# A layer's scale and shift, summed beside the mixers of the layer before

## The chip, the cores and the metric

The kernel runs on one core of a Trainium2 chip. The metric is the device time of one execution, in microseconds (us). TensorE is called PE here, VectorE DVE, ScalarE ACT, GpSimd POOL; SP is the engine whose queue issues all the loads and stores.

## The reference

Two layers of a small diffusion-style model in float32 work on 640 tokens of 2048 channels: 128 of a prompt ("context") and 512 of a sample. Every layer first modulates its input with a scale and a shift that come from a condition vector, one for the prompt and one for the sample, then mixes, then adds the gated output projection:

```python
def adaln(x, cond, norm_w, w_ada, b_ada):
    mod = jax.nn.silu(cond) @ w_ada + b_ada
    shift, scale, gate = jnp.split(mod, 3, axis=-1)
    return rmsnorm(x, norm_w) * (1 + scale) + shift, gate

for li in range(DEPTH):                        # 2
    hc, gate_c = adaln(xc, cc, norm_w[li], w_ada[li], b_ada[li])
    hl, gate_l = adaln(xl, cl, norm_w[li], w_ada[li], b_ada[li])
    if li % 2 == 0:
        ...                                    # mixers A (gated delta rule) and B (windowed attention)
    else:
        ...                                    # mixers C (gated linear attention) and D (neighbourhood attention)
    xc = xc + gate_c * (oc @ w_out)
    xl = xl + gate_l * (ol @ w_out)
```

`w_ada` of a layer is 2048 x 6144: 2048 columns each of shift (part 0), scale (part 1) and gate (part 2). Its product with two condition vectors depends on no token, so it can be made at any time before its use.

## The kernel before

The activations stand channel by channel: 16 tiles of [128 channels, 640 tokens], each split into a high and a low part (`hh`, `hl`), as every weight is (`w_hi`, `w_lo`), so that three fast products make one exact one. A projection's column tile takes 16 K-tiles x 3 products x 2 halves of 320 tokens. Its weights come in quarters of four K-tiles (256 KB, `weights`, L1048): loaded into `w_st`, rounded by ACT to `w_hi` (L1051), subtracted by DVE to `w_lo` (L1053), three quarters ahead.

The stages, in order of time: the start (norm and modulation of layer 0), the layer 0 mixers with their projections, the first out projection, the layer 1 mixers with theirs, the second out projection.

In the layer 0 mixers, `run` steps generators side by side: the inverses, scans, preparation, values, gates of mixer A, queries and heads of mixer B, and `gate`, which makes part 2 of layer 0's modulation with products of PE (`ada`). A generator yields the time that its next products have to wait (in a clock that the program itself counts, `self.now`) or a condition; the earlier in the list, the sooner served. Between them `Main` fills in a few products of a projection. PE's order is pinned to this program order (`keep_in_program_order`); the other engines' order is made by the framework's scheduler (`schedule_with_timeline_sim=True`). In mixer A, each of 8 heads needs small triangular inverses, made by a chain of small POOL instructions (`a_invert`, L489 to L497) between two trips through DRAM; `a_inverted` loads them back (L517 to L519), and `a_join` uses them first (`i_vps`). Then comes a scan over 10 chunks (tiles `a_st`, `a_s`, `a_vno`), whose steps go back and forth between PE, ACT and DVE.

`ada_vec` makes a part of the modulation without PE doing the big sum. For every K-tile of 128 rows it loads [128, width] of `w_ada` (L1308), and for either condition adds the tile times one number per row to a sum: as one DVE instruction (L1322; L1320 for the first K-tile), or as a product of ACT (L1325) that POOL adds (L1327). After 16 K-tiles, small products of PE sum over the partitions (`adv_ps`), DVE copies the result (L1338), `ada_out` turns it (`ada_t`) and puts it into place (`mod`). With width 512 a part has 4 groups of 16 steps.

In the first out projection, `out_proj` takes 16 column tiles; after each, DVE adds the gated product to the residual (L1521), ACT squares it (L1464), POOL sums the squares (L1465), and POOL multiplies by layer 1's scale as soon as that is known (`scaled`, L1425). Beside it run two `ada_vec` streams for layer 1, a step of both after every sixth (later third) piece of the projection: the scale (part 1), one condition on DVE and one on ACT and POOL, and the shift (part 0), both on DVE. `end` then norms, scales and shifts, and makes layer 1's `hh` and `hl` (L1764, L1765). Layer 1's gate (part 2) is made beside the layer 1 mixers by `ada_vec` with width 256, both conditions on DVE and a wait of 6 a step.

Of the kernel before, what the change touches and what calls it, by code (L numbers as in the profile page):

```python
# [13 lines left out]
PSUM = bass.MemoryType.PSUM  # L14
# [5 lines left out]
T = 640  # L20
# [5 lines left out]
# ---------------------------------------------------------------- host constants (shapes only)  # L26
# [24 lines left out]
def gate_table():  # L51
    """Sums over a chunk: to the row itself, for either orientation of a block, and over one half."""
    P = np.arange(128)
    half = P // 64
    same = (half[:, None] == half[None, :]).astype(np.float32)
    F = (P[:, None] <= P[None, :]) * same
    B = (P[:, None] >= P[None, :]) * same
    h0 = (half == 0)[:, None]
    t = [np.where(h0, F, B), np.where(h0, B, F), np.repeat(h0, 128, 1), np.repeat(~h0, 128, 1)]
    return np.ascontiguousarray(np.concatenate(t, 1).astype(np.float32))  # L60


# what goes with the constants: widths
# [8 lines left out]
class G:  # L72
    """What every part of the kernel shares."""

    def mm(self, out, lhsT, rhs, **kw):
        """A matrix product, kept behind the one before; self.now runs along with TensorE's time (us)."""
# [13 lines left out]
def rsqrt(g, pool, x, n, tag, bufs=1):  # L90
    """1/sqrt(x) by Newton steps on VectorE; x is [.., n], positive."""
    nc = g.nc
# [12 lines left out]
# ---------------------------------------------------------------- mixer A: gated delta rule  # L105
CP = 648          # 2 | 128 | 4 | 512 | 2
CL = 644          # 128 | 4 | 512


def a_tok(blk, half):  # L110
    """First token of the chunk in one half of a block: context chunks 0, 1; latent chunks b, 7 - b."""
    if blk == 0:
        return 64 * half
    return 128 + 64 * (blk - 1 if half == 0 else 8 - blk)


def by_block(lat, half):
    """[128, 4, 64] view, of [128, 512] latent columns in token order, of the chunks in one half of blocks 1-4."""
    v = lat.rearrange("p (b c) -> p b c", c=64)
    return v[:, 0:4] if half == 0 else v[:, 7:3:-1]  # L120


def a_gates(g, src, tri):
    """beta, g and their cumulated forms for all heads; src: [128, 640] tile, 0:64 to be summed over two groups of
    32 rows (beta dir head | g dir head)."""
# [17 lines left out]
    # log1p(e) = 2 atanh(e / (2 + e))  # L143
# [39 lines left out]
    # with a row for every block and head, to be spread over the partitions  # L183
# [20 lines left out]
def a_conv(g, h, which, src):  # L204
    """Projected tile (two PSUM halves of 320) -> 2 silu(conv) as [128, 640], tokens block by block."""
# [22 lines left out]
def silu2(g, src, pool, tag="zs", bufs=1):  # L228
    """2 silu of a projected tile (two PSUM halves of 320) -> [128, 640]."""
# [10 lines left out]
def a_prep(g, h, qT, kT):  # L240
    """A delta-rule head up to the inverses of its chunks, both directions; q, k come doubled."""
# [6 lines left out]
    # ---- sums of squares per token  # L248
# [8 lines left out]
    def gram(x):  # L257
        """The second against the first within every chunk."""
# [19 lines left out]
    # ---- per-token scalars, [128, 2 orientations, 5 blocks]  # L278
# [21 lines left out]
    # ---- decays: exp(gc[col] - gc[row]) on the allowed side, and the other sign for the forward triangles  # L300
# [16 lines left out]
    # ---- grams  # L317
# [11 lines left out]
def a_scan(g, S, vT, gates, st):  # L329
    """The scan over a head's chunks and its norm; returns o^T [128, 640] gated."""  # L330
# [7 lines left out]
    def turn(x, dst):  # L338
        """Token-major x, in two parts."""
# [12 lines left out]
    # ---- what a chunk takes of a state: k against the inverses, for every block and orientation  # L352
# [20 lines left out]
    # ---- scan over chunks  # L373
# [9 lines left out]
    def ahead(o, blk, r, zero=False):  # L383
        """What of a chunk does not wait for the state."""
# [5 lines left out]
    def step(o, blk, s, p, nxt):  # L390
        """One chunk of either direction; s: [128, 2 directions, 128] states, None for zero states."""
# [53 lines left out]
    # ---- norm over the head, per token  # L445
# [28 lines left out]
def a_invert(g, M):  # L474
    """lhsT tiles for the inverses of I - M, M strictly lower (transposed for the forward units)."""
# [29 lines left out]
def a_inverted(g, h, d1, d2):  # L505
    """Loads what a_invert left: lhsT tiles for the inverses, their diagonal blocks as they are, and the blocks of M
    below them."""
# [17 lines left out]
def a_join(g, Mo, Zt, X, between):  # L525
    """The blocks of the inverses that couple the two halves of a chunk; between: products to do meanwhile."""
# [31 lines left out]
def a_setup(g, es):  # L558
    """Pools and fixed tiles of mixer A."""
# [9 lines left out]
# ---------------------------------------------------------------- attention, shared by mixers B and D  # L569
def attn_probs(g, q, keys, adds, init, sink):  # L570
    """Of one block of 128 queries: softmax(q^T keys + adds) / 2, [128 q, keys].
    keys: [(AP [128 d, n], n)]; adds: [(c0, c1, AP [128 q, c1 - c0])]."""
# [21 lines left out]
    # P / (2 den): the gate comes doubled  # L594
# [11 lines left out]
def attn_out(g, S, vals):  # L606
    """Returns, after yields, [128 d, 128 q] (PSUM) = V^T S; vals: [AP [128 keys, 128 d]]."""
# [14 lines left out]
def attn_run(g, blocks):  # L622
    """blocks: [(arguments of attn_probs, vals, function of the output)]; the scores run one block ahead."""
# [10 lines left out]
def drain(g, dst, src, scale=None):  # L634
    """Two PSUM halves of 320 tokens -> [128, 640]."""
# [8 lines left out]
def token_major(g, vT, dst, blocks):  # L644
    """PE-transposes 128-column views of vT into dst[:, i]."""
# [9 lines left out]
# ---------------------------------------------------------------- mixer B: windowed GQA, sink, axial rotary  # L655
def b_rope(g, x):
    """Rotates the latent columns of x [128, 640] in place."""
# [36 lines left out]
def b_head(g, h, q, gates):  # L694
    """Puts the outputs in the place of the queries."""
# [35 lines left out]
def b_table():  # L731
    """cos, signed sin [128 channels, 512 tokens]; window masks [128 q, prev | cur | cache | next]."""
# [13 lines left out]
# ---------------------------------------------------------------- mixer D: neighbourhood attention  # L746
# [18 lines left out]
def d_head(g, h, q, k, vsrc, gates):  # L765
    """Puts the outputs in the place of the queries, then of the gates."""
# [49 lines left out]
def d_table():  # L816
    """Column masks [128 q = (r, c), 4 blocks x 32 key columns] | 128 zeros."""
# [12 lines left out]
def d_rpb(rpb):  # L830
    """[8 heads, 15, 31] -> [8, 128 q = (r, c), 8 key rows x 48]: the entry for key row kr and key column
    16 + (key column - query column base) of every query, zero outside."""
# [8 lines left out]
# ---------------------------------------------------------------- mixer C: gated linear attention  # L841
# [3 lines left out]
def c_table():  # L845
    """tri/16 for either direction [128, 128]; 2 I [128, 64]; per level, the [128, 64] mask of the pairs (s on partitions,
    c along the row)."""
# [22 lines left out]
def c_head(g, h, qsrc, ksrc, vsrc, gates, st):  # L870
    """vsrc: two."""
    nc, c, P = g.nc, g.c, g.pc1
    hd = slice(h * 128, h * 128 + 128)
    # ---- log-decays, token-major, and their cumulated sums, channel-major
# [27 lines left out]
    # ---- scores within a chunk: the diagonal (counted by both directions), then halves against halves  # L902
# [9 lines left out]
    def decayed(l):  # L912
        """Queries and keys against the decay at the middle of their 2 w tokens: forward the later half's queries and the
        earlier half's keys, backward the others."""
# [27 lines left out]
    # ---- v, token-major  # L942
# [7 lines left out]
    # ---- decays to the chunk's ends  # L950
# [16 lines left out]
    # ---- states at the chunks' starts, and outputs; backward first  # L967
# [14 lines left out]
    def out_block(b, sf, sb):  # L982
        """sf, sb: the states at the starts of the block's two chunks, either direction."""
# [35 lines left out]
    # ---- norm over the head, per token  # L1019
# [22 lines left out]
# ---------------------------------------------------------------- trunk  # L1042
def weights(g, dram, k0, k1):
    """K-tiles k0 to k1, four at most, of one 128-column tile of a weight [128, 16 x 128], as exact high and low parts."""
# [12 lines left out]
def narrow(g, dram, q):  # L1057
    """Quarter q of the K-tiles of a 32-column tile of a weight [128, 16 x 32]: [128, 4, 64], low parts behind high ones."""
# [10 lines left out]
class Main:  # L1069
    """The projections asked for, a few products at a time; weights are loaded ahead."""  # L1070
# [7 lines left out]
    def ask(self, dram, prio, now=False, n=None):  # L1078
        """For use with yield from: out^T [128 columns, 640 tokens] of one weight tile, as two PSUM halves."""
# [12 lines left out]
    def turns(self, drams):  # L1092
        """Some, by quarters in turn, the first half of the tokens first; the second one in the general PSUM."""
# [11 lines left out]
    def halves(self, drams):  # L1105
        """The last ones, of all of them the first half of the tokens first."""
# [28 lines left out]
    def narrow(self, r, q, wt):  # L1135
        """Of one of 32 columns a quarter of the K-tiles; the sums of the weights' high and low parts stay apart."""
# [12 lines left out]
    def work(self, r, k0, w):  # L1149
        """The K-tiles from k0 on for which w are the weights."""  # L1150
# [18 lines left out]
    def when(self):  # L1169
        """The time from which there is something to do."""  # L1170
# [20 lines left out]
    def until(self, ask, fill=None, every=1):  # L1191
        """The result of one that was asked for, with a step of fill between so many of its pieces."""
# [12 lines left out]
def run(g, main, *streams):  # L1205
    """Runs generators side by side, the first ones first; they yield how long (us) their next products have to
    wait, or a condition. The projections fill the time."""
# [17 lines left out]
def split(g, x, k, lo=None):  # L1225
    """High and low parts of x [128, 640] in the slots of k-tile k; lo: where x is already in its low part's."""
# [8 lines left out]
# projections of layer 0 that start before all of the modulation is there  # L1235
EARLY = [0, 8, 41, 43, 33]
# the mixers' outputs in the order in which they are done
# [738 lines left out]
```

## Time and profile before

| | us |
|---|---|
| median of 3 runs (2844.3 to 2858.61) | 2854.96 |
| span of the profiled execution | 2851.8 |
| busy: PE | 2682.8 |
| busy: DVE | 1654.9 |
| busy: ACT | 987.1 |
| busy: POOL | 781.3 |
| mean granted clock of PE | 0.970 of full speed |

The profiled execution's own time is its span; it lies 3.2 us below the median of the runs. A profile of one execution shows each instruction of each engine with its start and its length, what ended the idle time before it, and the clock that PE was granted. Rows name the line of the kernel, the engine, the operation and the tiles (out<-in). PE's matrix products are pipelined and their ends are modelled, so the time from one start to the next says more of PE's pace than its busy time does.

### The profile page before, as it was taken

The page shows a single profiled execution, that of the slowest core. Times are in us where ns is not written, and L with a number is a line of the kernel's source. Part 1 is how long each engine was busy: PE and PEld are TensorE (multiplying, and loading weights), DVE is VectorE, ACT ScalarE, POOL GpSimd, SP SyncE. Part 2 cuts the span into 40 slices and gives each one's busy share as a digit, 9 for nine tenths or more (in the row PEclk, how much of TensorE's full clock was granted, in tenths as well). Part 3 has the DMA queues.
Part 4 walks back from the last instruction along what each step waited for, and adds up shares of the span by engine and source line. Part 5 has one row for each costly group of instructions (what it writes and reads, how often), then busy time and mean ns, then how long its engine had stood idle before and what let it go on. Part 6 is the DMA issues. An engine that isn't in the chain of part 4 may idle for free.

```text
span 2851.8 us, 54254 instructions
## 1 busy us (share of the span) xinstructions
PE 2682.8 (94%) x20975; PEld 2464.5 (86%) x20975; DVE 1654.9 (58%) x3650; ACT 987.1 (35%) x2190; POOL 781.3 (27%) x930
## 2 busy tenths in 40 slices
PE   6979999999999999978889899999999999999997
PEld 5768788787888998978789898999799989979996
DVE  5665555556665754489997754446354535645225
ACT  3232342343333434343334542343233224324222
POOL 2325505134153350025553230022002001200223
PEclk9989999999999999998989999999999999999998
DMA  9933233232322221276663413223132313215223
GB/s 337 288 97 103 78 93 94 83 97 82 106 86 64 78 87 54 76 239 209 210 213 116 133 66 102 79 87 104 50 112 72 106 59 104 83 64 182 99 100 133
DMA packets 264705, 329.82 MB, mean 116 GB/s; under 512 B 76013, under 2 KB 148925, under 8 KB 264447
## 3 DMA queue, kind: packets, MB, share of 16 engines
q1 hardware_dynamic: 264447, 326.35, 35.3%
q8 instruction: 165, 2.70, 0.4%
q14 instruction: 93, 0.76, 0.1%
HBM read 294.95 MB, written 28.68 MB: 113 GB/s over the span
## 4 chain that ended last, share of the span: by engine, by line
PE 69%; DVE 10%; issue 9%; DMA 7%; POOL 2%; ACT 1%; SPq 1%; DVEq 0%; ACTq 0%; POOLq 0%
PE acc L77 54%; PE a_st L77 3%; DVE vec L1322 2%; DMA a_df<-gc_d 2%; PE c_ops L77 2%; PE at_s L77 2%; PE at_o L77 2%; DVE w_lo L1053 1%; PE c_U L77 1%; DMA adv<-w_ada 1%; PE ada_ps L77 1%; DVE scale L1322 1%; DVE hl L1765 1%; PE at_pt L84 1%; DMA scale<-w_ada 1%
## 5 line engine op out<-in xcount | busy, mean ns | idle before, releaser
L77 PE MATMUL acc<-hh,w_hi 128*128 128x320 f32 (+1 forms) x4544 | 1462.4, 323 | 46.4 <-DVE x L1521 41.9
L77 PE MATMUL acc<-hl,w_hi 128*128 128x320 f32 (+1 forms) x4544 | 1424.3, 314 | 8.6 <-DVE hl L1231 8.0
L77 PE MATMUL acc<-hh,w_lo 128*128 128x320 f32 x4480 | 1408.3, 314 | 9.8 <-DVE w_lo L1053 9.5
L77 PEld LDWEIGHTS acc<-hh,w_hi 128*128 128x128 f32 (+1 forms) x4544 | 866.5, 191 | 96.7 <-issue 76.8
L77 PEld LDWEIGHTS acc<-hl,w_hi 128*128 128x128 f32 (+1 forms) x4544 | 867.5, 191 | 16.4 <-DVE hl L1231 11.5
L77 PEld LDWEIGHTS acc<-hh,w_lo 128*128 128x128 f32 x4480 | 857.0, 191 | 17.4 <-DVE w_lo L1053 10.8
L1053 DVE TENSOR_TENSOR w_lo<-w_st,w_hi 128x512 fp32r<-128x512 f32 x561 | 430.0, 767 | 531.9 <-ACT w_hi L1051 528.2
L1051 ACT CAST w_hi<-w_st 128x512 fp32r<-128x512 f32 (+1 forms) x604 | 365.0, 604 | 823.2 <-PE acc L77 684.5
L1322 DVE SCALAR_TENSOR_TENSOR vec<-vec,cond 128x256 f32<-128x256 f32 (+1 forms) x360 | 250.4, 735 | 21.1 <-DMA vec<-w_ada 20.1
L495 POOL TENSOR_TENSOR i_S<-i_S,i_tmp 40x30 f32<-40x30 f32 (+14 forms) x240 | 144.4, 602 | 18.6
L493 POOL TENSOR_TENSOR i_tmp<-i_S 40x30 f32<-40x30 f32 (+14 forms) x240 | 134.8, 562 | 18.1
L1327 POOL TENSOR_TENSOR scale<-scale,scale_t 128x512 f32<-128x512 f32 x60 | 95.0, 1584 | 116.6 <-ACT scale_t L1325 103.5
L789 POOL TENSOR_TENSOR d_bias<-d_braw,d_mask 128x256 f32<-128x256 f32 x32 | 23.7, 772 | 359.7 <-PE tm_ps L84 359.7
L1465 POOL TENSOR_TENSOR n_acc<-n_acc,n_sq 128x640 f32<-128x640 f32 (+1 forms) x30 | 47.7, 1590 | 208.9 <-ACT n_sq L1464 208.9
L302 POOL TENSOR_TENSOR a_at<-a_df,consts 128x640 f32<-128x640 f32 x8 | 13.0, 1626 | 325.6 <-PE a_st L77 98.5
L77 PE MATMUL ada_ps<-adv,cond 128*32 128x128 f32 x1536 | 67.3, 297 | 26.0 <-DMA adv<-w_ada 24.1
L215 DVE SCALAR_TENSOR_TENSOR a_y<-a_pad,consts,a_y 128x644 f32<-128x644 f32 x96 | 90.0, 937 | 2.1
L922 POOL TENSOR_TENSOR c_X<-c_b 128x320 f32<-128x320 f32 x48 | 39.6, 825 | 175.9 <-PE c_lv L77 155.4
L77 PEld LDWEIGHTS ada_ps<-adv,cond 128*32 128x32 f32 x1536 | 38.9, 115 | 46.8 <-DVE n_acc L1465 19.5
L1325 ACT ACTIVATE scale_t<-scale,cond 128x512 f32<-128x512 f32 x60 | 43.0, 721 | 90.6 <-DMA scale<-w_ada 77.2
L1053 POOL TENSOR_TENSOR w_lo<-w_st,w_hi 128x256 fp32r<-128x256 f32 (+1 forms) x43 | 36.1, 844 | 103.7 <-ACT w_hi L1051 90.6
L887 POOL TENSOR_TENSOR c_gk<-c_gk,c_e 128x1280 f32<-128x1280 f32 x4 | 11.9, 2964 | 188.4 <-ACT c_e L886 188.4
(318 smaller groups left out, 2976.2 us busy)
## 6 DMA issues: line engine op xcount, KB each, us to landing
w_st<-w_in_odd SPq DMA_DIRECT2D x232, 256.0 KB
adv<-w_ada SPq DMA_DIRECT2D x192, 256.0 KB
w_st<-w_in_even SPq DMA_DIRECT2D x188, 256.0 KB
w_st<-w_out_even SPq DMA_DIRECT2D x72, 256.0 KB
w_st<-w_out_odd SPq DMA_DIRECT2D x72, 256.0 KB
scale<-w_ada SPq DMA_DIRECT2D x64, 256.0 KB
vec<-w_ada SPq DMA_DIRECT2D x64, 256.0 KB
vec<-w_ada SPq DMA_DIRECT2D x128, 128.0 KB
```

Of the source, the lines that this page charges most:

```text
L77: i = self.nc.tensor.matmul(out, lhsT=lhsT, rhs=rhs, **kw)
L84: i = self.nc.tensor.transpose(out, x, ident)
L215: nc.vector.scalar_tensor_tensor(out=y, in0=pad[:, j:j + CL], scalar=w[:, j:j + 1], in1=y, op0=ALU.mult, op1=ALU.add)
L493: E.tensor_tensor(out=t, in0=S[:, j + 1:, j].unsqueeze(2).to_broadcast([40, n, j]), in1=S[:, j, 0:j].unsqueeze(1).to_broadcast([40, n, j]) ...
L495: E.tensor_tensor(out=S[:, j + 1:, 0:j], in0=S[:, j + 1:, 0:j], in1=t, op=ALU.add)
L922: nc.gpsimd.tensor_tensor(out=pv(X[0])[:, :, 1 - d], in0=bv[:, :, 1 - d], in1=bm, op=ALU.subtract)
L1051: nc.scalar.copy(hi, st)
L1053: (nc.gpsimd if g.spare >= 0 else nc.vector).tensor_tensor(out=lo, in0=st, in1=hi, op=ALU.subtract)
L1322: nc.vector.scalar_tensor_tensor(out=acc[:, c], in0=st, scalar=sc, in1=acc[:, c], op0=ALU.mult, op1=ALU.add)
L1325: nc.scalar.activation(t, st, AF.Copy, scale=sc)
L1327: nc.gpsimd.tensor_tensor(out=acc[:, c], in0=acc[:, c], in1=t, op=ALU.add)
L1465: eng.tensor_add(accs[0][:, cs], accs[0][:, cs], t[:, cs])
```

## The change

The two streams leave the first out projection. In the layer 0 mixers a new generator, `ahead`, waits until two heads of mixer A are prepared and then makes part 1 and after it part 0 of layer 1's modulation with `ada_vec`, both conditions on DVE, a wait of 4 before each step. It has a store of its own (two sums and three K-tiles of width 512, where each of the old streams had four K-tiles), and it stands behind `gate` and ahead of the outputs' stream in the list. The products `adv_ps` and `ada_t` take PSUM tiles of the mixers' general pool, of which there are two, where the out projection's has four. The first out projection gets nothing to fill in, and the scale is there from its first tile on. A smaller scratch space for DMA descriptors leaves room in SBUF for the store.

```diff
@@ layer 0: mixers A and B
             g.pat = pool(e1, "pat")
+            g.pv = pool(e1, "pv")
...
             gate = ada(g, 0, (2,), [512] * (2048 // 512), ada_store(g.pa1, 1, 1, 512), 7)
+            store = vec_store(g.pv, 3, 1)
+
+            def ahead():
+                yield lambda: len(st["ready"]) >= 2
+                for part in (1, 0):
+                    yield from ada_vec(g, 1, part, store, ("dve", "dve"), 4)
+
             outs = g.outs = Outs(g, main, 53, I["w_out_even"], ORDER0, 2)
-            run(g, main, inverses(), scans(), first(), prep(), value(), bs(), queries(), zgate(), bgate(), gate, outs.stream())
+            run(g, main, inverses(), scans(), first(), prep(), value(), bs(), queries(), zgate(), bgate(), gate, ahead(), outs.stream())
...
-            steps = ada_vec(g, 1, 1, vec_store(px, 4, 2, name="scale"), ('dve', 'act'))
-            steps = side(steps, ada_vec(g, 1, 0, vec_store(px, 4, 2), ('dve', 'dve')))
             sh = mod(g, 1, 0)
...
-            out_proj(g, 0, outs, px, lambda n: I["xT"][n], lambda n: x1[n], steps,
-                     lambda n: g.mod[1, 1][:, n] if g.mods.get((1, 1), 0) > n else None, end)
+            out_proj(g, 0, outs, px, lambda n: I["xT"][n], lambda n: x1[n], (),
+                     lambda n: g.mod[1, 1][:, n], end)
...
-    nc = _bacc.Bacc("TRN2", target_bir_lowering=False, num_devices=1)
+    nc = _bacc.Bacc("TRN2", target_bir_lowering=False, num_devices=1, dynamic_dma_scratch_size=1024)
```

The rest of the diff takes comments out.

## The prediction

> **What bounds the kernel now.** I read the page's head and slices first: TensorE (PE) is busy nearly everywhere, so only a stretch in which it isn't, or in which its clock falls, can give time back. Around the 18th to 21st of the 40 slices PE falls to 7 and 8 tenths, the granted clock to 8 and 9, while DMA and VectorE (DVE) peak.
>
> ```profile
> span 2851.8 us, 54254 instructions
> PE   6979999999999999978889899999999999999997
> DVE  5665555556665754489997754446354535645225
> PEclk9989999999999999998989999999999999999998
> ```
>
> Then the busy times in stretches, in this order: start of the layer 0 mixers, their middle, the first out projection, and the steady part of the second. Columns: length, busy us (and instructions) of PE, PE's weight loads, DVE, ScalarE, POOL, then clock, DMA share, GB/s.
>
> ```profile
> 160.00:306.00 146.00, 121.01 (x1004) 109.89 (x1004) 95.10 (x230) 44.85 (x110) 56.95 (x74) 0.90 0.30 89
> 306.00:1100.00 794.00, 764.18 (x6778) 668.92 (x6775) 462.04 (x1159) 298.43 (x769) 287.61 (x451) 0.98 0.28 86
> 1243.00:1520.00 277.00, 229.93 (x1484) 224.96 (x1484) 260.70 (x310) 86.27 (x134) 145.32 (x98) 0.88 0.63 208
> 2606.00:2800.00 194.00, 194.00 (x1325) 194.00 (x1324) 59.67 (x104) 47.45 (x75) 37.06 (x39) 1.00 0.32 107
> ```
>
> In the first out projection DVE works 260.7 of 277 us, at clock 0.88; the second out projection, which has no such sums, keeps PE full at 1.00. The chain and the waits of that stretch name the same cause: PE waits for the residual on DVE (L1521), which stands behind the sums (L1322).
>
> ```profile
> by line: issue 25.3%; DVE vec L1322 21.7%; PE acc L77 15.8%; DVE scale L1322 8.7%; DMA scale<-w_ada 7.1%; DVE w_lo L1053 5.9%; DMA vec<-w_ada 4.0%; DVE x L1521 3.6%; DMA x_d<-x 2.2%; PE adv_ps L77 1.5%; DVE vec L1320 1.4%; DMA w_st<-w_out_e
> PE acc L77 <- DVE x L1521: 41.9, 12, 7.3
> PE acc L77 <- DVE w_lo L1053: 5.2, 1, 5.2
> ```
>
> **What it takes away.** From the first out projection go 64 K-steps of the scale and 64 of the shift: 192 DVE instructions on 512 columns, 64 of ScalarE, 60 of POOL, 128 loads of 256 KB on SP's queue, and eight small products with their eight spreads. The same stretch, by the products of the accumulators alone:
>
> ```profile
> 1243.00:1520.00 277.00, 225.37 (x1339) 219.97 (x1340) 16.23 (x41) 0.00 (x0) 0.88 0.63 208
> 2606.00:2800.00 194.00, 194.00 (x1325) 194.00 (x1324) 17.17 (x42) 0.00 (x0) 1.00 0.32 107
> ```
>
> The second out projection needs 194.00 / 1325 = 0.1464 us for one. At that pace 1339 take 196.0 us, so 81.0 of the 277.0 us can go. I leave the 5.2 us wait for w_lo, which is not the sums', and take **75.8 us**. The clock's recovery to 1.00 is inside this, since the pace was measured at 1.00. What is next there is PE itself: weights (w_lo), the residual and the POOL scaling are the same or lighter work than what the second projection hides. The bounds from below and above: 41.9 us (the waits alone, if the lower clock had another cause) and 81.0.
>
> **What it adds to the mixers.** 128 K-steps with two DVE instructions each: 240 multiply-adds and 16 first products on 512 columns (POOL and ScalarE get nothing now).
>
> ```profile
> L1322 DVE SCALAR_TENSOR_TENSOR scale<-scale,cond x60: 736/741/2059, 1248.6 to 1506.6; 128x512 f32<-128x512 f32 x60
> L1320 DVE TENSOR_SCALAR scale<-scale,cond x4: 471/476/983, 1248.0 to 1450.2; 128x512 f32<-128x512 f32 x4
> L1322 DVE SCALAR_TENSOR_TENSOR vec<-vec,cond 128x512 f32<-128x512 f32 x120 | 140.0, 1187 | 0.1
> L1327 POOL TENSOR_TENSOR scale<-scale,scale_t x60: 1267/1612/1869, 1248.8 to 1499.0; 128x512 f32<-128x512 f32 x60
> L1053 DVE TENSOR_TENSOR w_lo<-w_st,w_hi x142: 677/692/2324, 309.5 to 1095.5; 128x512 fp32r<-128x512 f32 x142
> ```
>
> Undisturbed one takes 0.741 us (median of the scale's 60); under POOL's constant adds the mean is 1.187. In the mixers POOL is busy 36% of the time (287.61 of 794); the nearest row is the like-sized w_lo there, median 0.692 and at worst 2.324. I take 0.80 us, hence 240 x 0.80 + 16 x 0.5 = **200 us of DVE**, with 185 (at 0.741 and 0.476) and 293 (at 1.187) as ends. DVE in the 794 us goes from 462 to 662, 83%: there is room, but not much.
>
> When they run: the stream starts once two heads are prepared (the second one's last product with M is at 306.1) and asks for 4 us a step. The gate's stream asks for 7, and its 64 steps lie between 168.6 and 824.6, 10.4 us each; scaled by 4/7 that is 5.9 us, so 128 steps and eight group ends last some 830 us, to about 1140: inside the mixers, which end before the out projection's first sum at 1248.6.
>
> ```profile
> L321 DVE TENSOR_TENSOR a_M<-a_gram,a_M x1: 825/825/825, 306.1 to 306.1; 128x640 f32<-128x640 f32 x1
> L1289 DVE TENSOR_TENSOR adv<-adv,ada_ps x60: 272/286/289, 168.6 to 824.6; 128x128 f32<-128x128 f32 x60
> ```
>
> But the steps won't be evenly spaced. Only PE is pinned to program order. In layer 1 the same function asks for 6 us a step, and its 32 instructions of a group come in bursts of 24 to 25 us with 90 us of nothing between (two bursts and the pause between them, first all work, then the stream's alone):
>
> ```profile
> 1719.00:1743.00 24.00, 24.00 (x167) 23.78 (x168) 17.40 (x42) 5.98 (x12) 0.00 (x0) 1.00 0.51 161
> 1834.00:1859.00 25.00, 25.00 (x189) 24.69 (x179) 20.04 (x48) 8.91 (x16) 0.00 (x0) 1.00 0.45 143
> 1719.00:1743.00 24.00, 0.28 (x4) 0.20 (x4) 13.81 (x33) 1.00 0.51 161
> 1743.00:1834.00 91.00, 0.26 (x16) 0.27 (x16) 0.00 (x0) 1.00 0.19 65
> 1834.00:1859.00 25.00, 0.45 (x16) 0.20 (x5) 13.90 (x33) 1.00 0.45 143
> ```
>
> So I expect eight bursts of 25 us of DVE, filling its gaps for about 60 us each (42% of it is free), the first perhaps before 306, where DVE is at 65% (95.10 of 146). Their price to PE is shown nowhere; the ends are these. Lower: nothing, as in those layer 1 bursts, where DVE stood at 73% and 80% and PE was full at 1.00. Upper: the first out projection itself, where 81.0 us were lost to the stream's 212 us of DVE (vec 146.30, scale 65.63), 0.38 us each; 200 x 0.38 = 76. The layer 0 mixers differ from layer 1 in that their scan already waits now and then for DVE and ScalarE:
>
> ```profile
> 1243.00:1520.00 277.00, 3.95 (x72) 3.04 (x72) 146.30 (x132) 0.88 0.63 208
> 1243.00:1520.00 277.00, 3.71 (x72) 2.84 (x72) 65.63 (x68) 45.79 (x64) 95.01 (x60) 0.88 0.63 208
> PE a_st L77 <- ACT a_vno L411: 12.6, 5, 5.5
> PE a_st L77 <- DVE a_s L426: 6.1, 3, 3.0
> ```
>
> I take half of the upper end, 0.18 x 200 = **36 us**: the load lies between the two, and a pinned PE can't go round a late scan step.
>
> The small products (3.95 + 3.71 us of PE there, and their spreads) move into PE's full time: **9 us**. They take one of two PSUM buffers of the general kind instead of one of four; the gate's products take such a buffer 64 times now, and their longest entry among PE's waits of the middle stretch is 1.1 us, so nothing is added.
>
> ```profile
> PE ada_ps L77 <- ACT i_Vn L537: 1.1, 3, 0.4
> ```
>
> SP: the 128 loads move into a queue where the weights' loads (L1048) stand behind them, and a load waits for a buffer that a multiply-add frees (three buffers, not four). Layer 1's bursts have that too and cost nothing, and the DMA engines have room (share 0.28 in the middle stretch). If that cover went, a weight would be late by one multiply-add pair, 1.6 us; I put that inside the 36.
>
> POOL's inverses are the other neighbour: 30 products and 30 sums a head, one after another, then a turned copy; for the third head from 442.66 to 485.84.
>
> ```profile
> L495 POOL TENSOR_TENSOR i_S<-i_S,i_tmp x210: 242/594/1237, 314.1 to 1041.1; 40x30 f32<-40x30 f32 x7, 40x84 f32<-40x84 f32 x7, 40x130 f32<-40x130 f32 x7, 40x168 f32<-40x168 f32 x7
> 442.66 0.15 POOL L489 MEMSET i_S<- 40x32 f32 x1 [17.16 <-DMA i_S<-inv_in]
> 482.29 3.55 POOL L497 TENSOR_TENSOR i_S<-i_S,consts 40x1024 f32<-40x1024 f32 x1
> 495.08 0.44 SPq L518 DMA_DIRECT2D a_Zt<-inv_out  x1
> 504.85 0.82 PE L77 MATMUL i_vps<-i_X,i_M 32*32 32x32 f32 x40
> ```
>
> The last load of its inverse goes out at 495.08 and PE uses it at 504.85: some 9 us of slack. A burst that falls on a chain stretches it (594 median, 1237 at worst now); I charge **6 us** in all.
>
> **The sum**: 75.8 - 36 - 9 - 6 = 24.8 us off the profiled execution's 2851.8, 2827.0. The median of the runs shown is 3.2 us above that span, so I predict **2830**.
>
> [...]
>
> **The rivals.**
> 1. *Hidden altogether* (0.2): as in layer 1, bursts cost PE nothing. Then 75.8 - 9 = 66.8 off: 2788. For it: PE 24.00 of 24.00 in a burst. Against: there POOL did nothing in it, and the scan waits above.
> 2. *Slower by POOL* (0.2): the inverses and the multiply-adds take turns, so a burst that meets a chain holds it up by 32 x 0.74 = 23.7 us; beyond 9 us of slack that is 15 us of PE's time each, 118 for 8 heads. With 40% to 60% of the chains met, 47 to 71: 75.8 - 36 - 9 - 47 = -16 or, with 71, -40, so 2871 to 2895. It decides against the change once stalls pass 75.8 - 36 - 9 = 31 us, a quarter of the 118. For it: the inverse's instructions reach twice their median even now (1237 and 594). Against: POOL's adds beside a full DVE in the out projection were 1.612 by the median and 1.267 at least, a quarter longer, not twice; a quarter of 43 us is 11, 2 beyond the slack.
> 3. *A wash* (0.2): with DVE at 83%, and near 100% in bursts, a pinned PE loses 0.3 us for each us of DVE, nearer to the out projection's 0.38: 75.8 - 60 - 9 - 6 = 0.8, so 2854.
> 4. *The change doesn't take*: the stream starts late and spills into the out projection. The 100 us between 1140 and 1248 speak against it; if a quarter spilled, a quarter of the 75.8 would go, 19 us: 2849, inside the range.
>
> **How the numbers follow.** Forecast (2805 to 2845) 0.4, rival 1 0.2, rival 2 0.2, rival 3 0.2. A difference under 0.5% (14 us) is what a measurement can't tell from none: 2840.7 to 2869.2. Faster: rival 1, and most of the forecast (0.36): 0.56. Same: 0.04 of the forecast and 0.18 of rival 3: 0.22. Slower: 0.22. The range, 2784 to 2882, leaves out a tenth on each side; the likeliest case's own is 2805 to 2845.
>
> **What would show it.** Right: the first out projection's stretch at clock 1.00 with DVE near 55 us, no wait for L1521, its 1339 products in some 200 us instead of 277; L1322 in eight bursts between about 200 and 1140; PE's waits in the mixers up by some 40 us, on a_st and at_s. Wrong: waits of PE on i_vps of 10 us or more (rival 2), or the out projection's start late by as much as it gains (rival 3), or L1322 still in the out projection (4).

## The result, and the profile after

The changed kernel takes 2895.66 us (median of four runs, 2889.92 to 2902.52) against 2851.97 of the kernel before in the runs beside it: a ratio of 1.0146, 95% interval [1.0128, 1.0165]. It is slower by 1.5%. Its profiled execution spans 2888.1 us. The page's head and slices:

```profile
span 2888.1 us, 54046 instructions
PE   6968998899897978999999899999999999999997
DVE  5776567867766769445334854356354535545225
PEclk9979998999998989999999999999999999999998
```

The hole in slices 18 to 21 is gone, as forecast. New small ones stand in slices 3, 13 and 15, inside the layer 0 mixers (a slice is 72 us). The busy times in stretches; first the changed kernel's mixers and its first out projection:

```profile
160.00:1360.00 1200.00, 1056.00 (x8900) 934.88 (x8899) 808.39 (x1864) 409.63 (x1047) 373.04 (x526) 0.94 0.36 107
1360.00:1575.00 215.00, 215.00 (x1461) 214.81 (x1460) 70.13 (x113) 52.78 (x84) 42.84 (x46) 0.99 0.37 121
```

and the mixers of the kernel before:

```profile
160.00:1243.00 1083.00, 1021.33 (x8789) 909.80 (x8788) 634.34 (x1593) 409.96 (x1050) 349.21 (x528) 0.97 0.29 88
```

The out projection gave back what was promised: PE is full and the clock 0.99. I take the start of the last `at_o` product of layer 0 as the mixers' end (1242.7 us before, 1359.5 after) and the first `n_ss` product of `end` as the out projection's. The out projection went from 295.0 to 215.3 us, and what follows took 1314.1 and 1313.3. So the whole difference is -79.7 in the out projection and **+116.8 in the mixers**. There PE's idle time rose from 61.7 (1083 - 1021.33) to 144.0 us, and its busy time by 34.7 at a lower clock, 0.94.

PE's waits over the mixers, after:

```profile
PE a_st L77 <- ACT a_vno L411: 30.2, 15, 4.8
PE a_ops L84 <- ACT a_oraw L456: 27.5, 5, 16.5
PE gc_ps L77 <- DVE g_or L168: 15.8, 1, 15.8
PE at_pt L84 <- DVE at_S L602: 14.7, 5, 7.6
...
PE i_vps L77 <- DMA i_X<-inv_out: 0.4, 1, 0.4
```

and before:

```profile
PE a_st L77 <- ACT a_vno L411: 15.8, 6, 5.5
...
PE at_pt L84 <- DVE at_S L602: 3.6, 3, 2.5
...
PE gc_ps L77 <- DVE g_or L168: 1.6, 1, 1.6
...
PE a_ops L84 <- ACT a_oraw L456: 0.7, 1, 0.7
```

The inverses (`i_vps`) are not late at all. What is late comes at the ends of chains of short DVE instructions, in which each needs the result of the one before it: the gates' (`g_or`), the softmax's (`at_S`), and the norm before `a_ops`, 58.0 us together against 5.9 before. The scan's wait (`a_vno`) has grown too, by 14.4. The timeline of DVE up to the end of an 8.1 us wait of PE (883.0 to 891.1 us) for one of these norms (start, length, then line, operation and tiles):

```profile
869.95 0.56 DVE L96 TENSOR_SCALAR a_rho_y<-a_rt 128x5 int32<-128x5 int32 x1
870.42 0.74 DVE L1322 SCALAR_TENSOR_TENSOR vec<-vec,cond 128x512 f32<-128x512 f32 x1
871.08 0.74 DVE L587 CUSTOM_DVE_ANT_0 at_S<-at_s,b_tab,consts 128x512 f32<-128x512 f32 x1
871.75 0.08 DVE L587 DVE_READ_ACCUMULATOR2_ANT at_mx<- 128x1 f32 x1
871.75 0.48 DVE L97 TENSOR_SCALAR a_rho_y<-a_rho_y 128x5 int32<-128x5 int32 x1
872.15 1.66 DVE L1322 SCALAR_TENSOR_TENSOR vec<-vec,cond 128x512 f32<-128x512 f32 x2
873.73 0.14 DVE L591 TENSOR_SCALAR at_nm<-at_mx 128x1 f32<-128x1 f32 x1
873.79 0.44 DVE L99 TENSOR_TENSOR a_rho_t<-a_rho_y 128x5 f32<-128x5 f32 x1
...
884.18 0.21 DVE L101 SCALAR_TENSOR_TENSOR a_rho_y<-a_rho_t,a_rho_y 128x5 f32<-128x5 f32 x1
884.30 0.15 DVE L601 RECIPROCAL at_den<-at_den 128x1 f32<-128x1 f32 x1
884.38 3.98 DVE L1322 SCALAR_TENSOR_TENSOR vec<-vec,cond 128x512 f32<-128x512 f32 x2
888.28 0.15 DVE L99 TENSOR_TENSOR a_rho_t<-a_rho_y 128x5 f32<-128x5 f32 x1
```

Every instruction of `a_rho` needs the one before it. Before the change such a chain, from L96 to the last L101, ran in 3.9 us:

```profile
930.23 0.48 DVE L96 TENSOR_SCALAR a_rho_y<-a_rt 128x5 int32<-128x5 int32 x1
930.75 0.17 DVE L97 TENSOR_SCALAR a_rho_y<-a_rho_y 128x5 int32<-128x5 int32 x1
...
933.70 0.39 DVE L101 SCALAR_TENSOR_TENSOR a_rho_y<-a_rho_t,a_rho_y 128x5 f32<-128x5 f32 x1
```

Now it takes 20.5 us (869.95 to 890.43), since a multiply-add or two has been put into nearly every link (from one instruction of the chain to the next). The sums come in eight bursts; four of them as stretches (columns as before the change: length, busy us of PE, its weight loads, DVE, ScalarE, POOL, then clock, DMA share, GB/s):

```profile
156.00:201.00 45.00, 23.96 (x140) 20.93 (x138) 44.41 (x89) 11.80 (x30) 9.66 (x8) 0.71 0.55 172
648.00:683.00 35.00, 31.64 (x296) 29.19 (x295) 31.83 (x58) 11.11 (x27) 0.00 (x0) 0.95 0.60 189
864.00:907.00 43.00, 23.48 (x152) 20.95 (x147) 37.36 (x75) 8.96 (x26) 21.77 (x27) 0.76 0.46 131
983.00:1028.00 45.00, 33.43 (x245) 28.54 (x234) 44.36 (x67) 9.74 (x28) 41.32 (x50) 0.92 0.43 129
```

Where PE waits long for a chain (the first, at `gc_ps`, and the third), it works 24 of 45 and 23 of 43 us and its granted clock falls to 0.71 and 0.76; in the second, with no wait over 3 us, PE keeps 31.64 of 35 and 0.95. One such wait by itself: PE stands still from 1020.9 to 1037.4 us, for `a_ops`, and the granted clock is 1.00 from 1016 to 1020.9, 0.50 from 1025 to 1037 and 1.00 again from 1042 to 1060.

### The profile page after: what moved, and what is told of

It is laid out like the page before. It is cut to its first block, busy times and chain, and to the rows that moved or that the text cites. A ratio compares the mean times of both kernels' runs of the same rounds, so it can differ in the third digit from the quotient of the medians.

```text
span 2888.1 us, 54046 instructions
## 1 busy us (share of the span) xinstructions
PE 2683.5 (93%) x20975; PEld 2461.6 (85%) x20975; DVE 1632.1 (57%) x3714; ACT 947.4 (33%) x2126; POOL 698.1 (24%) x870
## 4 chain that ended last, share of the span: by engine, by line
PE 70%; issue 10%; DVE 10%; DMA 6%; POOL 2%; ACT 1%; SPq 1%; DVEq 0%; ACTq 0%; POOLq 0%
PE acc L77 56%; PE a_st L77 3%; DVE vec L1322 3%; PE c_ops L77 2%; DMA a_df<-gc_d 2%; PE at_s L77 1%; PE at_o L77 1%; PE c_U L77 1%; DVE w_lo L1053 1%; PE ada_ps L77 1%; POOL i_S L495 1%; DMA adv<-w_ada 1%; DMA hl<-o_d 1%; PE at_pt L84 1%; POOL i_tmp L493 1%
## 5 line engine op out<-in xcount | busy, mean ns | idle before, releaser
L1322 DVE SCALAR_TENSOR_TENSOR vec<-vec,cond 128x512 f32<-128x512 f32 (+1 forms) x480 | 301.1, 665 | 31.1 <-DMA vec<-w_ada 29.0
L495 POOL TENSOR_TENSOR i_S<-i_S,i_tmp 40x30 f32<-40x30 f32 (+14 forms) x240 | 154.1, 642 | 18.7
L493 POOL TENSOR_TENSOR i_tmp<-i_S 40x30 f32<-40x30 f32 (+14 forms) x240 | 150.9, 629 | 17.9
L1521 DVE SCALAR_TENSOR_TENSOR x<-acc,mod,x_old 128x128 f32<-128x128 f32 (+2 forms) x96 | 39.2, 437 | 49.4 <-PE acc L77 47.9
L593 ACT ACTIVATE at_S<-at_S,at_nm 128x384 f32<-128x384 f32 (+2 forms) x80 | 47.6, 595 | 50.2 <-DVE at_nm L591 49.8
L77 PE MATMUL a_st<-a_vno,a_at 64*64 64x128 f32 x320 | 32.7, 282 | 30.2 <-ACT a_vno L411 30.2
```

The lines of the kernel that those rows point to most:

```text
L77: i = self.nc.tensor.matmul(out, lhsT=lhsT, rhs=rhs, **kw)
L493: E.tensor_tensor(out=t, in0=S[:, j + 1:, j].unsqueeze(2).to_broadcast([40, n, j]), in1=S[:, j, 0:j].unsqueeze(1).to_broadcast([40, n, j]) ...
L495: E.tensor_tensor(out=S[:, j + 1:, 0:j], in0=S[:, j + 1:, 0:j], in1=t, op=ALU.add)
L593: nc.scalar.activation(S[:, 0:n], S[:, 0:n], AF.Exp, bias=nm, accum_out=den[:, 0:1])
L1322: nc.vector.scalar_tensor_tensor(out=acc[:, c], in0=st, scalar=sc, in1=acc[:, c], op0=ALU.mult, op1=ALU.add)
L1521: nc.vector.scalar_tensor_tensor(out=xs[n][:, c0:c1], in0=ps[t][:, c0 - t * 320:c1 - t * 320], scalar=gate[:, n, cd:cd + 1], in1=xos[n][:, ...
```

## The experiments

Four theories. A: the multiply-adds get between the links of DVE's dependent chains. B: the loads on SP's queue. C: the group ends, with their small products and their PSUM buffers. P: contention with POOL. All ratios are to the kernel before, run on the same chip. The kernels are edits of the changed kernel unless the text says otherwise.

**Three terms taken one at a time.** `e1_narrow` leaves the sums of 496 of 512 columns out:

```diff
- nc.vector.scalar_tensor_tensor(out=acc[:, c], in0=st, ..., in1=acc[:, c], ...)
+ w8 = cols or width
+ nc.vector.scalar_tensor_tensor(out=acc[:, c, 0:w8], in0=st[:, 0:w8], ..., in1=acc[:, c, 0:w8], ...)
...
- yield from ada_vec(g, 1, part, store, ("dve", "dve"), 4)
+ yield from ada_vec(g, 1, part, store, ("dve", "dve"), 4, 16)
```

> The changed kernel, but its 240 multiply-adds in the mixers work on 16 of the 512 columns (layer 1's scale and shift are left incomplete); the number of instructions, the loads and the small products stay. Theory A (VectorE's time: whole multiply-adds stand between the dependent VectorE instructions of the mixers): the mixers lose about 20 us instead of 117, the out projection keeps its 80 us gain, so about 2790. Rival B (the loads on SP's queue and the DMA engines): nothing changes, about 2890. Rival C (the small products in PE's pinned order, the buffers and places in SBUF): about 2890 as well.

2809.56 us, 0.9835 [0.9817, 0.9852]; the mixers end 35.4 us later than before, not 117, but not the 20 that A expected either. The length of the sums carries most of the price. The 35 us are shared by all that stays: the short multiply-adds, the loads and the small products.

`e2_noload` leaves out all but the first three loads of either part (`if i < min(len(todo), most)`, with `most` at 3):

> The changed kernel, but only the first three K-tiles of either part are loaded in the mixers (scale and shift are wrong then); all 256 VectorE instructions stay at full width. Theory A: as slow as the changed kernel, 2880 to 2895, perhaps more, since the bursts get denser. Rival B (loads): about 2790.

2886.87, 1.0107 [1.0089, 1.0125]: beside full sums the loads are worth 8 to 9 us (the mixers end 8.3 us earlier than in the changed kernel).

`e4_noinv` leaves out 28 of the 30 steps of every inverse, in both kernels (`for j in range(1, 3)`):

> The kernel before with the same cut of POOL's inverses (30 steps to 2). The inverses have slack there, so 2835 to 2852 is expected by either theory; it is the base for the run beside it.

> The changed kernel with POOL's inverses cut from 30 steps a head to 2 (the inverses are wrong then), so that POOL hardly works in the mixers. To be read against the same cut in the kernel before. Rival P (POOL's instructions and the multiply-adds hold each other up): the difference between the two falls from +36 us to about 0 or below. Theory A (VectorE's own time in the gaps of its dependent chains): the difference stays above +20 us.

2831.18 (0.9921 [0.9905, 0.9938]) and 2856.64 (1.0016 [1.0006, 1.0026]): without the inverses the change still costs 25.5 us of 43.7. For theory P, some 18 us go with the inverses, not the whole.

**Order.** `e3_pinned` keeps the 256 DVE instructions of the stream in program order:

```diff
- nc.vector.scalar_tensor_tensor(out=acc[:, c], ...)
+ i_ = nc.vector.scalar_tensor_tensor(out=acc[:, c], ...)
+ if pin:
+     g.tc.keep_in_program_order(i_)
```

> The changed kernel, with each of the stream's 256 VectorE instructions kept behind the VectorE instruction that the program issues before it, so that the scheduler cannot move them forward into a burst. Same work, same loads. Theory A in its sharper form (the harm is in the bursts, where one or two multiply-adds stand in every gap of a dependent chain): the mixers lose about half, some 55 us, so 2825 to 2840. If it is VectorE's total time alone, whatever its place: still about 2890. Rival B: about 2890.

2838.44, 0.9935 [0.9919, 0.995]. The same sums (201 us of DVE) now cost the mixers 64.6 us, and the kernel is faster than before. The instruction's row after and pinned (count, shortest, median and longest ns, first and last start):

```profile
L1322 DVE SCALAR_TENSOR_TENSOR vec<-vec,cond x240: 728/746/3328, 157.8 to 1142.6; 128x512 f32<-128x512 f32 x120
```

```profile
L1324 DVE SCALAR_TENSOR_TENSOR vec<-vec,cond x240: 736/747/3465, 316.3 to 1152.3; 128x512 f32<-128x512 f32 x120
```

Pinned, the first multiply-add starts at 316 us, where the program asks for it (two heads prepared); unpinned, the scheduler had brought it forward to 158. I counted the multiply-adds that start between two neighbouring instructions of one reciprocal root (L96 to L101, 160 links in the mixers): none before, 30 after, 2 pinned; the links' gaps sum to 23.5, 59.6 and 34.7 us. All 30 stand in three of the 16 roots, those that fell into a burst. PE's waits, pinned:

```profile
PE a_st L77 <- ACT a_vno L411: 33.2, 19, 7.1
PE a_ops L84 <- ACT a_oraw L456: 10.4, 3, 4.9
PE at_pt L84 <- DVE at_S L602: 5.7, 5, 2.8
...
PE gc_ps L77 <- DVE g_or L168: 1.4, 1, 1.4
```

The three waits at the ends of the chains are 17.5 us together, against 58.0 unpinned: 40.5 us of the 41.9 by which PE's idle time in the mixers falls (144.0 to 102.1). The scan's wait for `a_vno` is not cured by the order; it is as long as unpinned.

`e9_first_pinned` pins the first group alone (`16 if part else 0` steps):

> As the changed kernel, but only the 32 instructions of the first of eight groups (the burst at 156 to 200 us) are pinned in program order. Theory A: the 16 to 20 us that the mixers' first stretch is longer (the gates' polynomial stretched by the burst, gc_ps at 204.6 instead of 184.6 us) come back: gc_ps at 183 to 188, the mixers end at 1340 to 1346, 2870 to 2880. Rival (that stall is absorbed by a later one): gc_ps early again, but the mixers still end at 1355 to 1362 and the time stays at 2885 to 2900.

2877.44, 1.0089 [1.0073, 1.0105]: `gc_ps` is back at 184.4 us from 204.6, and the median fell by 18, into A's range. In the profiled execution the mixers' end came only 6.8 us earlier (1352.7), later than A expected (1340 to 1346) and earlier than the rival did (1355 to 1362); that execution is the slowest of the four (2885.34). How much of this burst's price later waits take up stays open.

`e10_short` cuts the chains themselves in both kernels, one Newton step of the reciprocal root for three (L98) and one term of the gates' polynomial for five:

> The kernel before with the same cut of VectorE's chains (one Newton step instead of three, one polynomial term instead of five), as the base for the changed kernel with that cut: 2840 to 2855, 0 to 12 us less than the kernel before, since only PE's waits on a_rho, at_S and the gates are shortened.

> The changed kernel with VectorE's chains of dependent short instructions cut down: each reciprocal root does one Newton step instead of three, the gates' polynomial one term instead of five, so less of the work is there and the values are less exact. Theory A (each link of such a chain has a multiply-add put into it): the changed kernel gains far more from this than the kernel before with the same cut; the difference between the two falls from some 40 us to about 10 (0 to 20). Rival (VectorE's occupancy as such is the price): the difference stays at 30 us or more.

2838.02 (0.9942 [0.9927, 0.9957]) and 2871.0 (1.006 [1.0047, 1.0073]): the difference fell from 43.7 to 33.0, not to 10: A's number did not come, the rival's did. The links cut out are some 11 us of the price; PE's waits at `a_ops` and `gc_ps` fell from 43.3 to 16.7 us, while the wait for the softmax's `at_S`, which was not cut, was 18.4 us (14.7 in the changed kernel). That the rival's cause is not the whole is shown by `e3_pinned` alone: the same occupancy, 57 us less.

**Density.** `e11_one_tile` and, with the scale alone, `e13_half_one_tile` hold one K-tile in the store, so that every pair has to wait for its own load:

```diff
- store = vec_store(g.pv, 3, 1)
+ store = vec_store(g.pv, 1, 1)
```

> As the changed kernel, but the store has one K-tile instead of three: a pair of multiply-adds must wait for its own load, so VectorE's work can come in bursts no denser than a pair per load, without any pinning. Theory A (dense bursts, filling the room between dependent instructions): the mixers end 50 to 80 us later than before instead of 117, 2825 to 2855. Rival (each us of the added work has its price, however it is spread): mixers +105 or more, 2880 or more. Third (loads that wait for their buffer hold back the weights behind them on SP's queue): waits of PE on w_hi or w_lo, 2900 or more.

> Scale alone on VectorE beside the layer 0 mixers with one K-tile in the store, shift on VectorE in the out projection. Theory A: mixers +25 to 40 instead of the 53 with three tiles, out projection 223, 2804 to 2820. Rival (spreading does nothing): 2833.

2903.11, 1.0175 [1.0157, 1.0193], and 2852.11, 0.9989 [0.9979, 0.9998]: no better, and for the half form 19 us worse than with three tiles (`e5_shift_back`, below). The first time is the third theory's, but not by its mechanism: PE waits for no `w_hi` or `w_lo` in these mixers. But this is no clean trial of density, as DVE's waits in `e11_one_tile` show:

```profile
DVE vec L1322 <- DMA vec<-w_ada: 100.7, 85, 5.5
```

DVE stands idle for 100.7 us, in 85 waits, at sums whose load has not landed (10.0 us in 10 in the changed kernel): one harm for another. (The three waits at the chains' ends do fall, from 58.0 to 27.8 us.) Whether thinner bursts alone would help stays open.

**What is left without sums.** Starting from the changed kernel, `e14_nothing` keeps the stream's steps and waits but none of its work (scale and shift are set to 1), `e15_loads_only` adds the 128 loads, `e16_ends_only` adds the group ends instead, `e12_no_sums` has loads, ends and the 16 first products, but none of the 240 multiply-adds (`for c in range(2 if k < most else 0)`, with `most` at 1). The first three get three switches, for loads, sums and ends; the call of `e15_loads_only`:

```diff
- yield from ada_vec(g, 1, part, store, ("dve", "dve"), 4)
+ yield from ada_vec(g, 1, part, store, ("dve", "dve"), 4, True, False, False)
```

> As the changed kernel with its 128 loads, group ends, small products and spreads, but without the 240 multiply-adds (only the 16 first products of each sum are made). It measures what is left of the change's price without VectorE's sums. Theory A: mixers end 15 to 25 us later than before, 2788 to 2800. Rival (small products and loads are a large part, as the 35 us left with 16 columns could mean): +30 to 40, 2805 or more.

> The changed kernel with the new stream's steps and waits in the list of generators, but with none of its work: no loads, no sums, no small products or spreads (the scale and shift are set to 1 by eight small writes of POOL). The mixers of the changed kernel without sums ended 38.6 us later than before. Theory O (the stream's place in the list shifts what the program puts where in PE's pinned order, and that order is worse): mixers still 15 to 30 us later, 2787 to 2805. Rival C (the loads and the small products cost it): mixers at 1240 to 1250, 2770 to 2780.

> As the one before, but with the 128 loads of 256 KB. Theory C with the loads: 8 to 20 us more than with nothing. Rival: within 5 us of it.

> As the one with nothing, but with the eight group ends: the small products, their copies and their spreads, on sums set to 1 once. Predicted for these were 9 us; theory C with the small products: 15 to 30 us more than with nothing. Theory O: 7 to 12 us more, PE's own time for them.

| kernel | median us | ratio | mixers end | over nothing |
|---|---|---|---|---|
| `e14_nothing` | 2774.03 | 0.9725 [0.971, 0.974] | 1240.3 | |
| `e16_ends_only` | 2781.26 | 0.9752 [0.9733, 0.9771] | 1246.8 | 6.5 |
| `e15_loads_only` | 2794.31 | 0.9801 [0.9781, 0.9821] | 1256.7 | 16.4 |
| `e12_no_sums` | 2812.1 | 0.9849 [0.9833, 0.9865] | 1281.3 | 41.0 |
| changed kernel | 2895.66 | 1.0146 [1.0128, 1.0165] | 1359.5 | 119.2 |

Theory O falls: the stream's place in the list costs nothing. The ends cost about what had been charged for PE's own time. `e12_no_sums` ends its mixers 38.6 us later than before, as its rival expected (30 to 40), not A. The loads alone cost 16, and this is where most of it shows. DVE prepares a head with a small array, `a_df`, that was written to DRAM and is loaded back (L251) on SP's queue. SP's queue in `e15_loads_only`, and below it DVE:

```profile
288.39 8.39 SPq L1308 DMA_DIRECT2D vec<-w_ada  x8
296.82 0.43 SPq L1048 DMA_DIRECT2D w_st<-w_in_even  x1
297.30 1.28 SPq L251 DMA_DIRECT2D a_df<-gc_d  x2
```

```profile
294.26 1.24 DVE L298 TENSOR_TENSOR a_c<-a_c,g_dl 128x10 f32<-128x10 f32 x1
307.53 0.82 DVE L301 TENSOR_TENSOR a_df<-a_df,a_gcu 128x640 f32<-128x640 f32 x1 [12.03 <-DMA a_df<-gc_d]
```

Eight loads of 256 KB go out ahead of it, in 8.4 us; DVE stands 12.03 us at `a_df` (5.3 at the longest of the eight in `e14_nothing`), the scan's next instruction (`a_vns`, L409) starts after it, at 309.08, and PE's wait for `a_vno` there is 11.1 us. `e12_no_sums` has a like stall at 566 us, in DVE's waits and in PE's:

```profile
DVE a_df L301 <- DMA a_df<-gc_d: 48.4, 8, 14.8
PE a_st L77 <- ACT a_vno L411: 28.2, 7, 15.2
```

There too `a_vns` starts after `a_df` (566.88 and 566.13 us). Why loads, ends and first products cost 18 us more together (41.0) than loads and ends do apart (22.9) is not shown: the waits that grew are spread over several tiles. In the changed kernel the longest wait at `a_df` is 5.6 us, probably because there the loads wait for the sums (SP's queue at L1308 for L1322: 104.9 us in 78 waits).

**Halves.** `e5_shift_back` makes the scale beside the mixers and the shift in the out projection, on DVE, as before; `e8_half_pinned` pins the scale's instructions as well:

```diff
- for part in (1, 0):
+ for part in (1,):
...
+ steps = ada_vec(g, 1, 0, vec_store(px, 4, 2), ('dve', 'dve'))
- out_proj(..., lambda n: x1[n], (), ...)
+ out_proj(..., lambda n: x1[n], steps, ...)
```

> Half of the change: the scale is summed by VectorE beside the mixers (4 bursts), the shift by VectorE during the first out projection as before. Theory A: the mixers lose half or less of the 117 us, 45 to 60; the out projection has 95 us of multiply-adds on a VectorE that has 215 - 70 us free, without POOL's adds, and keeps 65 to 78 of its 80 us: 2825 to 2845. If the out projection suffered from any such stream at all: about 2870.

> The scale alone stays beside the layer 0 mixers, on VectorE, with its 128 instructions pinned in program order; the shift is summed by VectorE in the out projection. Theory A (VectorE's bursts stand inside chains of dependent short instructions): pinned bursts cost PE about half of unpinned ones, so the mixers take 30 to 35 us more than before instead of the 53 us of the unpinned form, the out projection 222 to 226 us, and the time is about 2813 (2805 to 2822). Rival (the price is one of VectorE's occupancy, order does not matter for the scale alone): mixers +53, 2833 as without pinning.

2832.66, 0.9914 [0.9894, 0.9934], as A expected, and 2822.52, 0.9889 [0.987, 0.9907]. Pinned, the mixers take 40.4 us more than before instead of 53.1, the out projection 222.3; A had expected 30 to 35 for the mixers and a time just below this one. So for the scale alone order is worth a quarter of the price, not half: the long waits of the changed kernel at `a_ops` and `at_pt` (882 to 1037 us) stand beside bursts of the shift.

`e6_scale_pe` gives the scale to PE beside the mixers, as layer 0's gate is made, with the shift on DVE in the out projection; `e7_both_pe` gives both parts to PE beside the mixers (the cut of the code is of `e6_scale_pe`):

```diff
- store = vec_store(g.pv, 3, 1)
+ store = ada_store(g.pv, 2, 1, 512)
- yield from ada_vec(g, 1, part, store, ("dve", "dve"), 4)
+ yield from ada(g, 1, (1,), [512] * 4, store, 7)
```

> The scale is summed by TensorE beside the mixers (64 steps of four products, as the gate of layer 0 is), the shift by VectorE during the first out projection. Theory A: no multiply-adds in the mixers, so these lose only TensorE's 28 us and some waits, 30 to 40; the out projection keeps 65 to 78 us: 2805 to 2825, faster than the kernel before. If any third stream in the mixers costs what this change's did: 2870 or more.

> Both parts summed by TensorE beside the mixers, 4 us asked for between steps; nothing in the out projection. TensorE's 56 us and some waits, 60 to 75 in all, against the 80 us won: 2835 to 2850, by theory A. If VectorE's multiply-adds were not what cost: 2890.

2820.54, 0.9884 [0.9869, 0.9899], as expected, and 2857.94, 1.002 [1.0005, 1.0034], which is outside what was expected. Summing a part on PE costs the mixers some 40 us (36.8 for one, 85.9 for two), most of it PE's own time (its busy time there is 30.8 and 69.0 us above the 1021.0 of before), so one part pays and two don't. The out projection of `e6_scale_pe`, with half of the old load:

```profile
1280.00:1500.00 220.00, 217.61 (x1515) 215.29 (x1515) 163.96 (x248) 51.78 (x82) 48.41 (x44) 0.99 0.60 193
```

DVE works 164 of 220 us and PE loses next to nothing: one stream is hidden there. Whether the second one was too much by its DVE work or by POOL's adds is not separated. `e6_scale_pe` and `e8_half_pinned` beat both kernels, by 1.1 to 1.2% against before.

## Why the prediction was wrong

**What it takes away: right.** 75.8 us were predicted; the stretch gave 79.7, and the changed kernel without the stream's work stands at 2774.03 against 2851.01, 77 us. PE is next there, as said, at clock 0.99 with DVE at 70 us.

**How much DVE work, and when: right.** 200 us predicted; the 240 multiply-adds took 197.5 and the 16 first products 8.3, in eight bursts, the multiply-adds from 157.8 to 1142.6 us. They last 34 to 46 us each, not 60.

**Its price to PE: this step failed.** "I take half of the upper end, 0.18 x 200 = 36 us" (half of 0.38 would be 0.19, and 38). From `e12_no_sums` to the changed kernel the sums cost 83.6 us by the medians and 78.2 by the mixers' ends: 0.40 us for each us of DVE, past the 0.38 that I had called the upper end. The lower end was taken from layer 1, whose bursts left PE full; that showed that DVE at 73% and 80% need not hurt, but not that the work beside it has the same chains. The text named the scan as the difference and then averaged. It expected PE's waits at `a_st` and `at_s` to rise by some 40 us; PE's idle time rose by 82, and 52 of it stands at `a_ops`, `gc_ps` and `at_pt`.

What it left out is that the scheduler, free to order DVE, puts ready multiply-adds into the gaps of a chain: the one in the timeline above grew from 3.9 to 20.5 us, by one or two times 0.74 us in nearly every link. Pinned, the same sums cost 2838.44 - 2812.1 = 26 us, 0.13 each. (Both prices may be some 15 us too low, since the base, `e12_no_sums`, has long stalls at `a_df` that neither of the two has: 48.4 us of DVE's waits there against 33.6 unpinned and 31.8 pinned. The 57 us between the two don't hang on it.) So most of the price, 57 us, is one of order, not of occupancy; the loads can't be behind it, being worth 8 to 9 us beside unpinned sums. Of the 58.9 us by which PE's idle time rises from `e12_no_sums` (85.1) to the changed kernel (144.0), 50.8 are the three waits at the chains' ends (7.2 to 58.0). That idle time is three quarters of the sums' price; the rest is slower products (8917 take PE 1035.9 us in `e12_no_sums`, at clock 0.96, and 8900 take 1056.0 in the changed kernel, at 0.94).

**The loads: failed.** They were put inside the 36, as "late by one multiply-add pair, 1.6 us", with the weights as what stands behind. The weights weren't late; with the loads alone a small load was, by eight others: 16.4 us by the mixers' ends, 20.3 by the medians, and with group ends and first products some 11 to 18 more. In the changed kernel that long stall is absent, and the loads' 8 to 9 us have no row of their own.

**The small products: right**, 9 us predicted, 6.5 to 7.2 measured.

**POOL: the second rival's number came out, its mechanism didn't.** It gave 2871 to 2895 by late inverses, and 2895.66 was measured; but PE's wait at `i_vps` is 0.4 us in all, and the inverses' L495 has a median of 614 ns (594 before). It was the multiply-adds that suffered: a burst's mean is 0.73 us (23.3 us for 32) in the four between 420 and 800 us, beside which POOL works 0 to 6 us, and 0.86 to 0.96 in the last three, where it works 22 to 41. One by one: the 154 that overlap no POOL instruction take 753 ns at most, the 86 that do take 964 by the mean, which makes 19 us of DVE in all. The longest, 3.33 us from 885.03, stands in the timeline above; it overlaps the inverses' turned copy (L497, 884.44 to 887.81) and ends 0.55 us after it. Some 18 us went with the inverses, against 6 predicted. Where the two met it was the multiply-adds that paid, not the chain of inverses, as the rival's "turns" had it.

The forecast's own row for it was misread: 0.741 is no time alone but the median of a row that ran beside the same adds as the 1.187, which is a mean. The shift's row has a median of 0.744 and the scale's a mean of 1.034; in both the sums that overlap no POOL instruction take 0.740, those that do 1.475 and 1.292.

**The sum**: predicted 36 + 9 + 6 = 51 against 75.8; measured by the medians 83.6 (sums) + 20.3 (loads) + 7.2 (ends) + 10.5 (the last two together, with the first products) = 121.6 against 77. That is a loss of 44 where a gain of 25 was forecast. The terms are steps from one kernel to the next in one order; the loads come out smaller beside full sums.

## What to carry to other kernels

Here the price of extra work on an engine off the critical path was set by the chains of short dependent instructions that run there and by who orders them, more than by the engine's busy share. Before pricing a filler by share, count such chains in the stretch and ask whether the filler can get between their links. If the scheduler is free to bring it forward, pin it where the program wants it: here that turned a loss of 1.5% into a gain of 0.6%. And look for the small urgent load that ends up behind a prefetch in the same queue: here DVE stood 12.0 us at a load behind eight prefetches, 5.3 us at the longest without any.

## What was not expected of the hardware

A multiply-add on 16 columns took 231 ns by the median against 746 on 512: a thirty-second of the work for a third of the time. PE's granted clock fell to 0.71 over 45 us in which it had stood still for 21, and after the stall of 16.5 us that ended at 1037.4 it stayed at 0.50 for another 4 us of work, in which the products of `acc` follow each other every 0.27 us (0.147 before the stall), so this stall cost more than its length.

```profile
L1323 DVE SCALAR_TENSOR_TENSOR vec<-vec,cond x240: 221/231/2120, 158.6 to 1050.4; 128x16 f32<-128x16 f32 x120
```
